# Six places of a two-layer hybrid block rearranged: query norm, last folding, second statistics, context states, head exponents, rotations

## The chip, the cores and the metric

The kernel runs on one core of one Trainium2 chip. A core has five engines that run at once and meet only at semaphores: TensorE (PE; its weight loads are listed apart as PEld), VectorE (DVE), ScalarE (ACT), GpSimd (POOL) and SyncE (SP), which here starts most of the transfers. The metric is the time of one execution on the device in microseconds (us), lower is better; the time before is the median of three runs. All inputs are resident in the device's memory, all arithmetic of the reference is done in the kernel.

## The reference

Two layers of a block with 512 tokens (`x`, width 2048) and 256 context tokens (`ctx`). Each layer modulates a normed input with shift, scale and gate, which come from `silu(c) @ ada_w`; layer 0 mixes a pooling branch and a 12-head attention with low-rank queries and keys (MLA), layer 1 mixes a 4-head bidirectional mLSTM and a 16-head window attention. Cut to what matters here:

```python
for i in range(2):
    shift, scale, gate = split(silu(c) @ ada_w[i] + ada_b[i], 3)         # the context's likewise
    h  = rmsnorm(x,  norm_w[i]) * (1 + scale)   + shift
    hc = rmsnorm(xc, norm_w[i]) * (1 + scale_c) + shift_c
    y, yc = even_mix(h, hc, ...) if i == 0 else odd_mix(h, hc, ...)
    x = x + gate * y
    if i == 0: xc = xc + gate_c * yc
return rmsnorm(x, final_norm)

# even_mix
p_in, p_gate, c_q, c_kv, k_r, a_gate = split(h @ w_in, EV_SIZES)
q = (rmsnorm(c_q, q_norm) @ w_uq)            # 12 heads x (128 + 64 rotated)
k, v from rmsnorm(c_kv, kv_norm) @ w_ukv, k_r rotated
y = concat(pool(p_in) * silu(p_gate), attention(q, k, v) * silu(a_gate)) @ w_out

# odd_mix: the mLSTM starts from the state that the context leaves
C_new = decay * C + einsum('bhs,bhsv,bhsk->bhvk', w, v, k)               # w: gate weights
s     = (q @ k.T) * exp(dlog - m_t)
num   = exp(inter - m_t) * (C @ q) + s @ v
ym    = rmsnorm(num / den) * head_norm * sigmoid(o) * silu(z)
ya    = window_attention(rope(aq), rope(ak), av, ...) * silu(az)
y     = concat(ym, ya) @ w_out
```

## The kernel before

All is computed in float32 with tokens along the free axis. A product of two float32 operands is done as three TensorE products of rounded halves: `split(src, h, l)` has ScalarE write the rounded value `h` and VectorE (or the engine given as `low`) the rest `l = src - h`; `load_w` (L106) brings a piece of weights (raw ring of 3, halves rings of 4) and splits it. `tmode` (L307, L309) and `kmode` (L320) are the matmul loops over four row blocks of 128 of the inner dimension, `kq` in 0..3 over 2048; L307 writes 512 columns of the tokens, L309 256 of the context.

A planner orders each engine's instructions when the program is built: of those that are ready it takes the one that stands first in the program, unless a region marks its work with `tc.high_priority()`, or fixes the order of an engine with `tc.manual_schedule(engines=...)`, where instructions of that engine go out as written. On the chip each queue then runs strictly in the order that was fixed. Tiles come from pools; tiles of one tag share a number of buffers, and a new tile waits for a buffer. PSUM has eight banks; the tag "pm" holds two small tiles in most stages.

**First stage** (about 24 to 590 us): the projection `h @ w_in`, one `in_group` after another. Groups 2 and 3 give `c_q` (768 columns wide); `c_evac` copies them out and sums squares, the copies go to DRAM `cqd`, and only the factor of the norm, `rq`, is kept (L514 to L522). Beside the groups runs `Background`: units of the modulation product, 16 pieces of `ada_w` each, summed by VectorE (L187), transposed and reduced (`red`, L192, L193) and folded over partitions by a small matmul (`pb`, L199) whose result four small VectorE additions place (`ada_place`, L131). The folding of a unit stands 16 steps into the next; that of the last unit stands in `finish`, at the stage's end.

**MLA stage** (about 590 to 1000 us): `cqd` is read back, `c_norm` (L476 on) forms the row factors (`rows`, L253 on: six `dg` products and two copies), multiplies (L480) and splits, with POOL doing the subtractions. Then, under a fixed PE order, heads' scores alternate with fillers (`run(n)`: projections L641, L661 and products of the next stage). `HEAD` is the columns of one head's projection.

**Second layer's input** (about 1000 to 1380 us): output products `out0`, sums of squares, `stats1(0)` (tokens) and `stats1(1)` (context): `stat_mm` (L265), a square root, `rows`. `hx_chunks` is a generator, advanced by `out0`, that writes the normed tokens.

**mLSTM's preparation** (about 1380 to 1560 us): the gates (L1070 to L1185: cumulative sums, per direction `d` a transposition `prow` (L1131), a chain of running maxima on VectorE (L1133 to L1162), `ptr` (L1147) and a transposition back, `pmc` (L1165)); the value products `mv_group(h)`, four pieces `kq` of 72 matmuls (L320) each; and `ctx_state(h, vc)`, which for both directions weighs the context's values (`wv`, L1207), splits them (`wvh`, `wvl`) and multiplies with the context's keys (`pc0`, six matmuls of L1215, printed `pc` in the profile). All small products here share the tag "pm" with two buffers. Last comes the group `odw[5]`. Units 20 to 23 of `Background` run beside it.

**mLSTM heads** (about 1560 to 1840 us): for each head loads and splits (`m_q`, `m_kv`), the output gates' product `m_oz` (192 matmuls into all four "px" banks), then `m_head`: per direction a broadcast product `bc` (one of four "pm" banks), sums and exponentials (`X`, `iw`, `qi`), then scores and the sums over states.

**Window attention** (about 1840 to 2300 us): `wq_split` rotates the queries through `do_rope` (L328 to L335): VectorE swaps halves (`rsw`, L330) and multiplies (`rt1`, L332), POOL multiplies the swapped copy (L334), VectorE adds. ScalarE and VectorE split the result (`wq`, L1436, L1437). The matmuls of projections and of the output (L1449) are fillers beside the heads' scores. `z_load` (L1528 on) reads the mLSTM's result back and splits it: the rounded half on VectorE (L1534), the rest on POOL (L1535).

Of the kernel before, what the change touches and what calls it, by code (L numbers as in the profile page):

```python
# [8 lines left out]
F32 = mybir.dt.float32  # L9
# [29 lines left out]
def tile_hybrid_dit(ctx: ExitStack, tc: tile.TileContext, ts: dict, out: bass.AP, dbg=None, upto=99):  # L39
# [134 lines left out]
    def ada_vec_steps(u, pp, tp, nb, ttag, tbufs):  # L174

        both = u < 20
        acc = [tp.tile([P, 512], F32, name=f"acc{u}_{v}", tag=f"acc{v}", bufs=1) for v in range(2 if both else 1)]
        for kc in range(16):
            at = tp.tile([P, 512], F32, name=f"at{u}_{kc}", tag="ada", bufs=nb)
            DM.dma_start(at, ts["ada"][u, kc // 2][:, (kc % 2) * 512 : (kc % 2) * 512 + 512])  # L180
            if kc == 0:
                V.tensor_scalar(acc[0], at, st[:, kc, 0:1], None, op0=ALU.mult)
                if both:
                    S.mul(acc[1], at, st[:, kc, 1:2])
            else:
                for v, a in enumerate(acc):
                    V.scalar_tensor_tensor(a, at, st[:, kc, v : v + 1], a, op0=ALU.mult, op1=ALU.add)  # L187
            yield
        red = tiny.tile([P, 2, 16], F32, name="red", tag="red", bufs=2)
        for v in range(len(acc)):  # L190
            tr = tp.tile([P, 512], F32, name="atr", tag=ttag, bufs=tbufs)
            V.transpose(tr, acc[v])  # L192
            V.tensor_reduce(red[:, v, :], tr.rearrange("p (b r) -> p b r", r=32), axis=AX.X, op=ALU.add)  # L193
            yield

        def finish():
            n = len(acc)
            pb = pp.tile([32, 2, 16], F32, name=f"pb{u}", tag="pm")
            T.matmul(pb[:, :n, :], fold, red[:, :n, :], start=True, stop=True)  # L199
            ada_place(u, pb, n)  # L200

        return finish

    class Background:
# [5 lines left out]
        def steps(self, units, args):  # L210
            done = None
            for u in units:
                it = ada_vec_steps(u, *args)
                n = 0
                while True:
# [8 lines left out]
                    yield  # L224
            done()

# [3 lines left out]

        def finish(self):
            for _ in self.it:
                pass


# [91 lines left out]
    def do_rope(ps, r, tmp):  # L327

        sw = tmp("rsw", NX)
        V.stream_shuffle(sw, ps[:, :NX], SWAP)  # L330
        t1 = tmp("rt1", NX)
        V.tensor_tensor(t1, ps[:, :NX], rope[0], op=ALU.mult)  # L332
        t2 = tmp("rt2", NX)
# [179 lines left out]

    ssq = [ap_.tile([P, NT], F32, name="ssqc", tag="ssqc", bufs=1), 0]  # L514
    for g in range(2):
        px, pc = in_group(2 + g, steps=(2, 2))
        for b, r in enumerate(c_evac([(px[b], pc[:, b, :]) for b in range(2)], ssq)):
            G.dma_start(cqd[2 * g + b], r)
    p6 = pp.tile([P, 6], F32, name="cps6", tag="pm")
    stat_mm(p6, ssq[0], 6, 512)  # L520
    rq = cp.tile([P, 6], F32, name="rq")
    V.tensor_copy(rq, rstd_col(p6, 6, MLA_SCALE))  # L522

# [63 lines left out]
    for i in range(6):  # L587
# [5 lines left out]
        for b in range(2):  # L593
# [3 lines left out]
            G.dma_start(agd[2 * i + b], t)  # L597
    bg.finish()
    esA.close()
# [24 lines left out]

    raw = []
    for j in range(4):
        raw.append(tf("cqr"))
        DM.dma_start(raw[j], cqd[j])
    c_norm(raw, rq, cq, V_QN, tf, pp, G)

# [197 lines left out]
    with tc.manual_schedule(engines={mybir.EngineType.PE}):  # L828
        run(6 * HEAD + 1024)
        s_stage(units[0], 0)  # L830
        run(HEAD // 4)
        s_stage(units[0], 1)
        run(HEAD // 2)
# [100 lines left out]
    bg.finish()  # L934
    stats1(0)

    def hx_chunks():
        for j in range(KC):
            h_chunk(j, x1[j], ssq1, 12, 1, *((HX[j][i], None) for i in range(2)), Ring(tz, 3), (0,), G if j % 2 else V)
            if j % 4:  # L940
                yield
# [247 lines left out]

    def mv_group(h):  # L1190
        px, pc = new_px(2), new_pc()
        pv = [px[b // 2][:, 256 * (b % 2) : 256 * (b % 2) + 256] for b in range(4)]
        for kq in range(4):
# [4 lines left out]
            bg.step(3)  # L1198
            kmode([pc[:, b, :] for b in range(2)], w, kcs, HC, kq == 0, kq == 3, 2)
        vx_store(h, [p_.rearrange("p (a b) -> p a b", b=256) for p_ in px])  # L1200
        return vc_store([pc])

    def ctx_state(h, vc):
        for d in range(2):
            wv = cm.tile([P, 2, 258], F32, name="wv", tag="wv", bufs=1)
# [3 lines left out]
            wl = cm.tile([P, 2, 258], F32R, name="wvl", tag="wvl", bufs=1)  # L1209
            split(wv, wh, wl)  # L1210
            pc0 = pmt("pc0", [P, 258])
            for b in range(2):
# [4 lines left out]

    ctx_state(0, vc)
    for h in range(1, 4):
        ctx_state(h, mv_group(h))  # L1220

    px, pc = new_px(2), new_pc()
    for kq in range(4):
        w = load_w(odw[5, kq])
        bg.step(2)
        tmode(px, [pc[:, b, :] for b in range(2)], w, range(4 * kq, 4 * kq + 4), HX, HC, kq == 0, kq == 3)
    bg.finish()
# [84 lines left out]

    def m_head(h, q, kv, oz):
        q32, qh, ql = q
        kh, kl, vh, vl = kv
        bcs, Xs, qis = [], [], []
        for d in range(2):
# [14 lines left out]
            Xs.append(X)  # L1332
            qis.append((qih, qil))
        SD = [[], []]
        for s_ in range(4):
# [64 lines left out]
    for h in range(4):  # L1400
        q_, kv_ = m_q(h), m_kv(h)
        m_head(h, q_, kv_, m_oz(h))

# [125 lines left out]
    def z_load(j):  # L1529
        raw = wp.tile([P, 1024], F32, name="wraw", tag="wraw", bufs=3)  # L1530
        for i in range(2):
            DM.dma_start(raw[:, 512 * i : 512 * i + 512], z1d[j + i])
            h, l = Z[j + i]
            V.tensor_copy(h, raw[:, 512 * i : 512 * i + 512])  # L1534
            G.tensor_tensor(l, raw[:, 512 * i : 512 * i + 512], h, op=ALU.subtract)  # L1535

# [326 lines left out]
```

## Time and profile before

| what | value |
|---|---|
| runs shown | 2321.92, 2322.08, 2317.99 us; median 2321.92 |
| profiled execution | 2320.82 us, its span 2319.0 us |
| PE busy | 2232.1 us, 12984 matmuls |
| PEld busy | 1897.7 us |
| DVE busy | 1414.7 us, 2860 instructions |
| ACT busy | 922.0 us, 1872 instructions |
| POOL busy | 177.0 us, 213 instructions |
| moved by DMA | 311.24 MB, mean 134 GB/s |
| mean granted clock | 0.99 |

Busy times are sums over the span of one execution; engines overlap, so they do not add up to it. A row of the waits names the waiting instruction by engine, output tile and line, then the instruction that let it go, then the idle time in total, how often, and the longest. A row of the table by stretches gives for each engine its busy time and number of instructions, then the clock that TensorE was granted as a share of full speed, the DMA engines' share and the rate in GB/s. A row of the timeline gives start, duration, engine, line, operation, out<-in, shape, and in brackets the idle time before it with its releaser. Rows of one line's or tile's instructions give minimum, median and maximum in ns and the first and last start in us.

### The profile page before, as it was taken

The numbers are of one execution on the slowest core, as the hardware profiler recorded it, in microseconds if no ns is written. First come the engines' busy times: TensorE is split into PE (matmuls) and PEld (weight loads), VectorE is DVE, ScalarE is ACT, GpSimd is POOL, SyncE is SP. The second block draws the span as 40 slices with busy tenths as digits, with TensorE's granted clock in tenths as the row PEclk, the third lists the DMA queues.
The fourth block names the chain that finished last, engine by engine and source line by source line (L and its number), as shares of the span: only waits on it lengthen the run. The fifth ranks groups of instructions, "written<-read, shape, count | busy, mean of one in ns | idle before, by whom it ended". The sixth has DMA issues, their size and how long they took to land.

```text
span 2319.0 us, 34267 instructions
## 1 busy us (share of the span) xinstructions
PE 2232.1 (96%) x12984; PEld 1897.7 (82%) x12984; DVE 1414.7 (61%) x2860; ACT 922.0 (40%) x1872; POOL 177.0 (8%) x213
## 2 busy tenths in 40 slices
PE   5999999999899999999999999899999989999997
PEld 3678888788799999878888899898888878776886
DVE  4579432396666766788558525752555676778435
ACT  3232222121344444542225322223565656766433
POOL 0000000000100000011113000000000000003111
PEclk9999999999999999999999999999999999999998
DMA  9856323565211112276444321753233212113434
GB/s 385 320 201 193 111 83 121 198 224 168 78 53 53 58 55 69 96 262 223 151 156 151 96 100 69 255 163 120 93 99 100 96 55 73 64 62 121 136 114 141
DMA packets 118581, 311.24 MB, mean 134 GB/s; under 512 B 13676, under 2 KB 21356, under 8 KB 118416
## 3 DMA queue, kind: packets, MB, share of 16 engines
q1 hardware_dynamic: 111536, 281.73, 36.2%
q0 software_dynamic: 6880, 27.32, 3.1%
q8 instruction: 102, 1.67, 0.3%
q14 instruction: 63, 0.52, 0.1%
HBM read 279.37 MB, written 29.62 MB: 133 GB/s over the span
## 4 chain that ended last, share of the span: by engine, by line
PE 62%; DVE 6%; DMA 2%; issue 2%; ACT 1%; POOL 0%; DVEq 0%; SPq 0%; ACTq 0%; POOLq 0%
PE px L307 17%; PE px L320 10%; PE pj L641 5%; PE px L1449 5%; PE s L704 4%; PE pc L309 3%; PE om L747 3%; PE pc L320 2%; PE s L1449 2%; PE pj L661 2%; PE po L1368 2%; PE tp L729 2%; DMA at<-in_ada_dram 1%; PE wpt L1611 1%; DVE wl L109 1%
## 5 line engine op out<-in xcount | busy, mean ns | idle before, releaser
L108 ACT CAST wh<-wraw 128x512 fp32r<-128x512 f32 (+2 forms) x556 | 326.4, 591 | 881.3 <-PE pc L309 407.1
L109 DVE TENSOR_TENSOR wl<-wraw,wh 128x512 fp32r<-128x512 f32 (+2 forms) x556 | 371.2, 673 | 491.6 <-ACT wh L108 472.0
L187 DVE SCALAR_TENSOR_TENSOR acc<-at,st,acc 128x512 f32<-128x512 f32 x360 | 253.2, 755 | 23.6 <-DMA at<-in_ada_dram 22.5
L320 PE MATMUL px<-wh,hxh 128*128 128x512 f32 (+2 forms) x512 | 175.0, 342 | 0.0
L320 PE MATMUL px<-wl,hxh 128*128 128x512 f32 (+2 forms) x512 | 174.3, 340 | 0.0
L320 PE MATMUL px<-wh,hxl 128*128 128x512 f32 (+2 forms) x512 | 174.2, 340 | 0.0
L307 PE MATMUL px<-h0h,wh 128*128 128x512 f32 x384 | 153.0, 398 | 0.0
L307 PE MATMUL px<-h0h,wl 128*128 128x512 f32 x384 | 151.7, 395 | 0.1
L307 PE MATMUL px<-h0l,wh 128*128 128x512 f32 x384 | 151.7, 395 | 0.0
L309 PE MATMUL pc<-h0h,wl 128*128 128x256 f32 x400 | 112.6, 282 | 0.0
L309 PE MATMUL pc<-h0h,wh 128*128 128x256 f32 x400 | 112.4, 281 | 0.0
L309 PE MATMUL pc<-h0l,wh 128*128 128x256 f32 x400 | 112.4, 281 | 0.0
L320 PEld LDWEIGHTS px<-wh,hxh 128*128 128x128 f32 x512 | 96.8, 189 | 12.5 <-ACT sz L1292 1.0
L320 PEld LDWEIGHTS px<-wl,hxh 128*128 128x128 f32 x512 | 96.8, 189 | 11.3
L320 PEld LDWEIGHTS px<-wh,hxl 128*128 128x128 f32 x512 | 96.9, 189 | 11.0
L307 PEld LDWEIGHTS px<-h0h,wh 128*128 128x128 f32 x384 | 72.1, 188 | 23.1 <-ACT wh L108 4.2
L307 PE MATMUL px<-hxh,wh 128*128 128x512 f32 x224 | 89.5, 400 | 0.0
L307 PE MATMUL px<-zxl,wh 128*128 128x512 f32 x224 | 89.3, 399 | 0.0
L307 PE MATMUL px<-hxl,wh 128*128 128x512 f32 x224 | 89.2, 398 | 0.0
L307 PE MATMUL px<-hxh,wl 128*128 128x512 f32 x224 | 89.2, 398 | 0.0
L307 PE MATMUL px<-zxh,wl 128*128 128x512 f32 x224 | 88.7, 396 | 0.0
L307 PE MATMUL px<-zxh,wh 128*128 128x512 f32 x224 | 88.3, 394 | 0.0
(880 smaller groups left out, 6020.9 us busy)
## 6 DMA issues: line engine op xcount, KB each, us to landing
at<-in_ada_dram SPq DMA_DIRECT2D x256, 256.0 KB, 3.4
at<-in_ada_dram SPq DMA_DIRECT2D x64, 512.0 KB, 7.9
wraw<-in_od_in_dram SPq DMA_DIRECT2D x64, 512.0 KB, 3.5
wraw<-in_ev_in_dram SPq DMA_DIRECT2D x56, 512.0 KB, 4.2
wraw<-in_ev_out_dram SPq DMA_DIRECT2D x44, 512.0 KB, 3.9
wraw<-in_od_out_dram SPq DMA_DIRECT2D x36, 512.0 KB, 3.5
wraw<-in_od_oz_dram SPq DMA_DIRECT2D x32, 512.0 KB, 3.5
xt<-in_xT_dram SPq DMA_DIRECT2D x16, 384.0 KB, 7.4
```

Source lines behind the costliest of these rows:

```text
L108: S.copy(h, src)
L109: low.tensor_tensor(l, src, h, op=ALU.subtract)
L187: V.scalar_tensor_tensor(a, at, st[:, kc, v : v + 1], a, op0=ALU.mult, op1=ALU.add)
L307: T.matmul(px[b], w_, Hx[kc][r_], start=s0, stop=s1)
L309: T.matmul(pc[b], w_, Hc[kc][r_], start=s0 and b == 0, stop=s1, skip_group_check=True)
L320: T.matmul(p_, h_, w_, start=s0, stop=s1, skip_group_check=True)
L641: T.matmul(t, w_, r_[:, sl], start=kc == 0 and n == 0, stop=kc == 3 and n == 2)
L661: T.matmul(t[:, b * 256 : (b + 1) * 256], h_, w_, start=kc == 0 and n == 0 and b == 0, stop=kc == 3 and n == 2, skip_group_check=True)
L704: T.matmul(s[:, c0 - k0 : c1 - k0], l_, r_[:, c0:c1], start=n == 0, stop=n == 4)
L729: T.transpose(tp[:, b * P : (b + 1) * P], pr[:, (b0 + b) * P : (b0 + b + 1) * P], ident)
L747: T.matmul(o[:, :256], v_[:, 6 - nk + b, :], p_[:, b, :], start=b == 0 and n == 0, stop=b == nk - 1 and n == 2)
L1449: T.matmul(px[b], w_, Hs[kc][r_], start=first and i == 0 and n == 0, stop=last and i == len(kcs) - 1 and n == 2)
```

## The change

- **Query norm**: in the first stage, behind group 3, `rows` is called and the four products with `q_norm` are done in place on the copies in `raw`; only then do they go to `cqd`. The MLA stage loads them and splits them, with VectorE as `low`.
- **Last folding**: `finish` of `Background` can leave the last unit's folding out; it is called by `bg.last(pp)` behind the first quarter of a head's filler in the MLA stage, with that stage's PSUM pool.
- **Second statistics**: `stats1(0)` moves from ahead of the last three output products into `hx_chunks`, which first advances behind the first `kq` of the first of them.
- **Context states**: `ctx_state` becomes a generator that stops ahead of each direction's products. `mv_group` advances the state of the head before behind `kq` 0 and `kq` 2, and so does the group `odw[5]` for the last head. These groups and the states' products stand under a fixed PE order, as written.
- **Head exponents**: the first half of `m_head` becomes `m_pre`, called before `m_oz`.
- **Rotations**: the swap and the first product of `do_rope` are marked with high priority.
- Besides, `z_load` splits with ScalarE and VectorE in place of VectorE and POOL.

```diff
@@ -193,9 +193,9 @@
             V.tensor_reduce(red[:, v, :], tr.rearrange("p (b r) -> p b r", r=32), axis=AX.X, op=ALU.add)
             yield
 
-        def finish():
+        def finish(pool=None):
             n = len(acc)
-            pb = pp.tile([32, 2, 16], F32, name=f"pb{u}", tag="pm")
+            pb = (pool or pp).tile([32, 2, 16], F32, name=f"pb{u}", tag="pm")
             T.matmul(pb[:, :n, :], fold, red[:, :n, :], start=True, stop=True)
             ada_place(u, pb, n)
 
@@ -222,15 +222,17 @@
                     if n == 16 and done:
                         done()
                     yield
-            done()
+            self.last = done
 
         def step(self, n=1):
             for _ in range(n):
                 next(self.it, None)
 
-        def finish(self):
+        def finish(self, fold=True):
             for _ in self.it:
                 pass
+            if fold:
+                self.last()
 
 
     def rstd_col(ps6, nb, mul=None, bufs=2):
@@ -327,9 +329,10 @@
     def do_rope(ps, r, tmp):
 
         sw = tmp("rsw", NX)
-        V.stream_shuffle(sw, ps[:, :NX], SWAP)
         t1 = tmp("rt1", NX)
-        V.tensor_tensor(t1, ps[:, :NX], rope[0], op=ALU.mult)
+        with tc.high_priority():
+            V.stream_shuffle(sw, ps[:, :NX], SWAP)
+            V.tensor_tensor(t1, ps[:, :NX], rope[0], op=ALU.mult)
         t2 = tmp("rt2", NX)
         G.tensor_tensor(t2, sw, rope[1], op=ALU.mult)
         V.tensor_tensor(r[:, :NX], t1, t2, op=ALU.add)
@@ -512,14 +515,16 @@
 
 
     ssq = [ap_.tile([P, NT], F32, name="ssqc", tag="ssqc", bufs=1), 0]
+    raw = []
     for g in range(2):
         px, pc = in_group(2 + g, steps=(2, 2))
-        for b, r in enumerate(c_evac([(px[b], pc[:, b, :]) for b in range(2)], ssq)):
-            G.dma_start(cqd[2 * g + b], r)
+        raw += c_evac([(px[b], pc[:, b, :]) for b in range(2)], ssq)
     p6 = pp.tile([P, 6], F32, name="cps6", tag="pm")
     stat_mm(p6, ssq[0], 6, 512)
-    rq = cp.tile([P, 6], F32, name="rq")
-    V.tensor_copy(rq, rstd_col(p6, 6, MLA_SCALE))
+    rb = rows(rstd_col(p6, 6, MLA_SCALE), 6, pp, ta("rstdb"))
+    for j in range(4):
+        V.scalar_tensor_tensor(raw[j], raw[j], vec[:, V_QN + j : V_QN + j + 1], rb, op0=ALU.mult, op1=ALU.mult)
+        G.dma_start(cqd[j], raw[j])
 
 
     m = NP - 16
@@ -595,7 +600,7 @@
             S.activation(t[:, :NX], px[b], AF.Silu)
             S.activation(t[:, NX:], pc[:, b, :], AF.Silu)
             G.dma_start(agd[2 * i + b], t)
-    bg.finish()
+    bg.finish(fold=False)
     esA.close()
     es0.close()
 
@@ -622,11 +627,10 @@
     def tf(name, n=NT):
         return mp.tile([P, NT], F32, name=name, tag="tf", bufs=11)[:, :n]
 
-    raw = []
     for j in range(4):
-        raw.append(tf("cqr"))
-        DM.dma_start(raw[j], cqd[j])
-    c_norm(raw, rq, cq, V_QN, tf, pp, G)
+        r = tf("cqr")
+        DM.dma_start(r, cqd[j])
+        split(r, *cq[j])
 
     heads = [dict() for _ in range(12)]
 
@@ -829,6 +833,7 @@
         run(6 * HEAD + 1024)
         s_stage(units[0], 0)
         run(HEAD // 4)
+        bg.last(pp)
         s_stage(units[0], 1)
         run(HEAD // 2)
         for i, un in enumerate(units):
@@ -932,9 +937,9 @@
     hxp = opool(ehx, "hx", side="right")
     HX = [(hxp.tile([P, NX], F32R, name=f"hxh{j}"), hxp.tile([P, NX], F32R, name=f"hxl{j}")) for j in range(KC)]
     bg.finish()
-    stats1(0)
 
     def hx_chunks():
+        stats1(0)
         for j in range(KC):
             h_chunk(j, x1[j], ssq1, 12, 1, *((HX[j][i], None) for i in range(2)), Ring(tz, 3), (0,), G if j % 2 else V)
             if j % 4:
@@ -1187,7 +1192,7 @@
     bg = Background(range(20, 24), pp, opool(ea, "ada1"), 4, "atr", 1)
 
 
-    def mv_group(h):
+    def mv_group(h, state):
         px, pc = new_px(2), new_pc()
         pv = [px[b // 2][:, 256 * (b % 2) : 256 * (b % 2) + 256] for b in range(4)]
         for kq in range(4):
@@ -1197,10 +1202,13 @@
             kmode(pv, w, kcs, HX, kq == 0, kq == 3, 2)
             bg.step(3)
             kmode([pc[:, b, :] for b in range(2)], w, kcs, HC, kq == 0, kq == 3, 2)
+            if kq % 2 == 0:
+                next(state, None)
         vx_store(h, [p_.rearrange("p (a b) -> p a b", b=256) for p_ in px])
         return vc_store([pc])
 
     def ctx_state(h, vc):
+
         for d in range(2):
             wv = cm.tile([P, 2, 258], F32, name="wv", tag="wv", bufs=1)
             for b in range(2):
@@ -1208,6 +1216,7 @@
             wh = cm.tile([P, 2, 258], F32R, name="wvh", tag="wvh", bufs=1)
             wl = cm.tile([P, 2, 258], F32R, name="wvl", tag="wvl", bufs=1)
             split(wv, wh, wl)
+            yield
             pc0 = pmt("pc0", [P, 258])
             for b in range(2):
                 kh, kl = (m_[:, b, h * P : (h + 1) * P] for m_ in mkc)
@@ -1215,15 +1224,22 @@
                     T.matmul(pc0, k_, w_[:, b, :], start=b == 0 and n == 0, stop=b == 1 and n == 2)
             split(pc0, C0[4 * d + h][0], C0[4 * d + h][1])
 
-    ctx_state(0, vc)
-    for h in range(1, 4):
-        ctx_state(h, mv_group(h))
+    state = ctx_state(0, vc)
+    next(state)
+    with tc.manual_schedule(engines={mybir.EngineType.PE}):
+        for h in range(1, 4):
+            vc = mv_group(h, state)
+            state = ctx_state(h, vc)
+            next(state)
 
     px, pc = new_px(2), new_pc()
     for kq in range(4):
         w = load_w(odw[5, kq])
         bg.step(2)
-        tmode(px, [pc[:, b, :] for b in range(2)], w, range(4 * kq, 4 * kq + 4), HX, HC, kq == 0, kq == 3)
+        with tc.manual_schedule(engines={mybir.EngineType.PE}):
+            tmode(px, [pc[:, b, :] for b in range(2)], w, range(4 * kq, 4 * kq + 4), HX, HC, kq == 0, kq == 3)
+            if kq % 2 == 0:
+                next(state, None)
     bg.finish()
     ea.close()
     for b in range(2):
@@ -1310,9 +1326,8 @@
             split(vr, vh[:, 2 * b : 2 * b + 2, :256], vl[:, 2 * b : 2 * b + 2, :256])
         return kh, kl, vh, vl
 
-    def m_head(h, q, kv, oz):
-        q32, qh, ql = q
-        kh, kl, vh, vl = kv
+    def m_pre(h, q32):
+
         bcs, Xs, qis = [], [], []
         for d in range(2):
             bc = pm4("bc", [P, 512])
@@ -1331,6 +1346,12 @@
             bcs.append(bc4)
             Xs.append(X)
             qis.append((qih, qil))
+        return bcs, Xs, qis
+
+    def m_head(h, q, kv, pre, oz):
+        q32, qh, ql = q
+        kh, kl, vh, vl = kv
+        bcs, Xs, qis = pre
         SD = [[], []]
         for s_ in range(4):
             sc = pm4("sc", [P, 512])
@@ -1399,7 +1420,7 @@
 
     for h in range(4):
         q_, kv_ = m_q(h), m_kv(h)
-        m_head(h, q_, kv_, m_oz(h))
+        m_head(h, q_, kv_, m_pre(h, q_[0]), m_oz(h))
 
     for b, px in enumerate(x_group_t(G_AQ)):
         S.copy(aq0[b], px)
@@ -1531,8 +1552,7 @@
         for i in range(2):
             DM.dma_start(raw[:, 512 * i : 512 * i + 512], z1d[j + i])
             h, l = Z[j + i]
-            V.tensor_copy(h, raw[:, 512 * i : 512 * i + 512])
-            G.tensor_tensor(l, raw[:, 512 * i : 512 * i + 512], h, op=ALU.subtract)
+            split(raw[:, 512 * i : 512 * i + 512], h, l)
 
     def fillers():
```

## The prediction

> **What bounds the kernel now.** The profile page comes first: how long the span is and which engine fills it.
>
> ```profile
> span 2319.0 us, 34267 instructions
> PE 2232.1 (96%) x12984; PEld 1897.7 (82%) x12984; DVE 1414.7 (61%) x2860; ACT 922.0 (40%) x1872; POOL 177.0 (8%) x213
> ```
>
> TensorE (PE) is busy for 2232.1 of 2319.0 us and nothing else passes 61% apart from its own weight loads. So the end moves by what PE waits for, and by the clock it runs at, and by little else. Work taken off VectorE (DVE), ScalarE (ACT) or GpSimd (POOL) is worth something only where PE waits for it. The second view is the list of PE's waits (instruction, releaser; total us, times, longest):
>
> ```profile
> PE ps L265 <- DVE rb L392: 23.4, 1, 23.4
> PE pc L1215 <- ACT wvh L108: 6.6, 2, 6.2
> PE px L1449 <- ACT az L1407: 4.2, 1, 4.2
> PE pj L641 <- DVE vl L109: 3.2, 1, 3.2
> PE pb L199 <- DVE red L193: 3.1, 1, 3.1
> PE ps6b L265 <- DVE ssq L885: 3.0, 1, 3.0
> PE px L1449 <- DVE rt L332: 1.9, 1, 1.9
> ```
>
> The 23.4 us are the start-up and are not touched. The next six are 22.0 us in all (6.6 + 4.2 + 3.2 + 3.1 + 3.0 + 1.9), under 1% of the span. A wait has a tail, though. The table by stretches, cut from PE's restart after each, shows it (start and end, us, busy of PE, PEld, DVE, ACT, POOL, then the granted clock):
>
> ```profile
> 591.20:597.00 5.80, 5.80 (x28) 5.74 (x29) 2.37 (x9) 0.00 (x0) 0.00 (x0) 0.51 1.00 357
> 610.20:614.00 3.80, 3.80 (x16) 3.51 (x17) 1.60 (x4) 1.08 (x3) 1.19 (x1) 0.55 0.21 69
> 1507.20:1511.70 4.50, 4.44 (x21) 4.44 (x22) 3.49 (x8) 0.83 (x3) 0.00 (x0) 0.51 0.90 277
> 1870.30:1873.50 3.20, 3.17 (x11) 2.68 (x12) 0.69 (x1) 0.77 (x2) 0.00 (x0) 0.51 0.26 63
> 1909.50:1914.50 5.00, 4.96 (x17) 3.92 (x18) 4.90 (x10) 3.77 (x6) 0.00 (x0) 0.66 0.19 50
> ```
>
> PE is full in each, at about half clock. Length times (1 - clock) is lost: 5.8 x 0.49 = 2.8, 3.8 x 0.45 = 1.7, 4.5 x 0.49 = 2.2, 3.2 x 0.49 = 1.6, 5.0 x 0.34 = 1.7 us. I count these 10.0 us as part of the waits. The Trainium skill (TensorE: Matmul & The Clock Gate, "HAM oscillation — how this bites in real kernels") asks for no idle gap of TensorE over about 3.4 us. By that rule the gaps of 3.1, 3.2 and 1.9 us would leave no tail, and 2.8 + 1.7 + 1.7 = 6.2 us of gain would drop out of the sum. The trace disagrees: the clock falls behind each of them, so the measurement decides.
>
> **Query norm.** PE's 3.2 us wait is for a value split `vl`, and DVE's timeline shows why that is late:
>
> ```profile
> 606.01 3.68 DVE L109 TENSOR_TENSOR wl<-wraw,wh 128x256 fp32r<-128x256 f32 x2
> 609.61 0.41 DVE L109 TENSOR_TENSOR vl<-pj,vh 128x256 fp32r<-128x256 f32 x1
> 602.48 8.91 POOL L109 TENSOR_TENSOR cql<-cnt,cqh 128x768 fp32r<-128x768 f32 x4 [12.34 <-ACT cqh L108]
> L480 DVE SCALAR_TENSOR_TENSOR cnt<-cqr,vec,rstdb x4: 1007/1008/1981, 600.0 to 603.8; 128x768 f32<-128x768 f32 x4
> ```
>
> Two `wl` take 3.68 us while POOL runs the four `cql` subtractions; the `vl` after them takes 0.41. Before that stand four `cnt` products of 1.0 to 2.0 us. The change moves the products, with the row statistics (six small matmuls, two copies), into the first stage, and gives the subtractions to DVE. There the moved work has room:
>
> ```profile
> 240.00:258.00 18.00, 18.00 (x107) 15.65 (x107) 9.72 (x23) 2.79 (x6) 1.26 (x2) 1.00 0.52 170
> 1227.00:1235.00 8.00, 7.73 (x64) 7.38 (x63) 4.89 (x12) 3.65 (x6) 0.00 (x0) 1.00 0.49 168
> ```
>
> DVE is busy 9.72 of 18 us where four products of 1.0 us and two copies are added; PE is full and goes on with the next group. I cost it at nothing; without that cover it is at most those four products plus copies, about 5 us. The four `cqd` stores now follow the norm, but they are read 350 us later. At the MLA stage DVE has four subtractions of estimated 1.0 us (an operation of that size, L480, takes 1.0) in place of four products of 1.0 to 2.0, with POOL silent. `vl` then comes before PE needs it: **-3.2 - 1.7 = -4.9**.
>
> **Last unit's folding.** The 3.1 us wait goes, since the fold matmul stands after a quarter head of filler. Next late is the PSUM bank of the gate group, on which PE's next product lands:
>
> ```profile
> 588.40 0.65 ACT L596 ACTIVATE sag<-pc 128x256 f32<-128x256 f32 x2
> ```
>
> It is read until 589.05, and PE is out of matmuls at 588.0: some 1.1 us stay, too short for a tail by the rows above. **-2.0 - 2.8 = -4.8**. Its four small additions now run on DVE at a point where it is not late.
>
> **Second statistics.** The call moved is that of the first half (near 1232 us). There PE is busy 7.73 of 8 us (row of 1227 above), so nothing is to be won; the wait of 3.0 us (`ps6b`) belongs to the second half's call, which stays. **0**, within 1 us either way.
>
> **Context states.** The 6.2 us wait with its tail goes: in the new order PE runs another quarter of the next group (72 matmuls; 0.124 us each by the row of L320 below, 8.9 us) before the state's product, while `wvh` was 6.2 late. **-6.6 - 2.2 = -8.8.** But the PE order is now fixed from the first state on: three quarters of group 1 stand behind the product of state 0. Rows of the gates' last transposes (L1165) and of that product (L1215: count, durations, first and last start), then of single instructions:
>
> ```profile
> L1165 PE MATMUL pmc<-con,Mr x8: 198/219/225, 1435.3 to 1449.4; 4*128 4x4 f32 x8
> L1215 PE MATMUL pc<-wvh,mkch x16: 282/335/583, 1449.5 to 1548.8; 128*128 128x258 f32 x16
> 1424.01 0.62 ACT L108 CAST wvh<-wv 128x516 fp32r<-128x516 f32 x1 [2.32 <-DVE wv L1207]
> 1424.79 0.68 DVE L109 TENSOR_TENSOR wvl<-wv,wvh 128x516 fp32r<-128x516 f32 x1
> 1426.80 0.19 DVE L1113 TENSOR_TENSOR rho<-II,beta 128x32 f32<-128x32 f32 x1
> 1429.27 0.14 DVE L1149 COPY tr<-ptr 4x4 f32<-4x4 f32 x1
> 1435.48 0.60 PE L1131 MATMUL prow<-con,rho 128*4 128x128 f32 x4
> 1449.20 0.41 PE L1165 MATMUL pmc<-con,Mr 4*128 4x4 f32 x4
> ```
>
> State 0's operands are ready at 1425.5, yet its product runs at 1449.54, right behind the last `pmc`. In the same way the second direction's `prow`, whose input is ready at 1427.0 and for which both buffers are free from 1429.41, runs at 1435.48, right behind the first `pmc`. All are tiles of one PSUM tag with two buffers. I read it as: that tag hands out its buffers in the order of the program, so state 0's product cannot start before the last `pmc`, which ends DVE's chain of running maxima. In before PE fills that time with group 1:
>
> ```profile
> 1431.00:1449.50 18.50, 17.14 (x138) 16.13 (x136) 1.00 0.21 72
> ```
>
> (matmuls of L320 alone). These 17.1 us of work (17.14 / 138 = 0.124 us each) would now stand behind the product. DVE could end its chain up to 2.7 us sooner, as four `wl` splits of that engine (0.67 each, as the `wvl` row above) lie within it; so 14.4 to 17.1, I take 15, and 2 for the clock after it (the tails above are 1.6 to 2.8). The other end is no cost at all, if the buffer comes free early. I take the stall, since two instructions show the same pattern. **+17 - 8.8 = +8.2.**
>
> **Head exponents.** They move ahead of the head's gate products. PE has no gap there:
>
> ```profile
> 1580.00:1840.00 260.00, 259.85 (x1283) 213.87 (x1283) 138.03 (x314) 146.14 (x365) 7.77 (x25) 1.00 0.30 99
> ```
>
> 0.15 us idle in 260. Nothing to win; two of four small PSUM buffers are held longer, which could cost up to 1.5 us. **0.**
>
> **Rotations.** The chain ahead of the 4.2 us wait:
>
> ```profile
> 1860.14 0.68 DVE L332 TENSOR_TENSOR rt<-aq,rope 128x512 f32<-128x512 f32 x1
> 1862.57 1.79 DVE L332 TENSOR_TENSOR rt<-aq,rope 128x512 f32<-128x512 f32 x1
> 1866.62 1.26 ACT L1436 CAST wq<-wrr 64x512 fp32r<-64x512 f32 x2 [2.62 <-DVE wrr L335]
> 1867.89 1.28 ACT L1407 ACT_TABLE_LOAD   x1
> 1869.19 1.09 ACT L1407 ACTIVATE az<-px 128x512 f32<-128x512 f32 x2
> 1908.81 0.68 DVE L332 TENSOR_TENSOR rt<-px,rope 128x512 f32<-128x512 f32 x1
> ```
>
> `rt` waits in DVE's queue, slowed to 1.79 beside POOL; `wrr`, `wq` follow, and ACT reaches the table load and `az`, which frees PE's bank, only after `wq`. With the shuffle and the product first in the queue the second `rt` would follow the first at once and without POOL beside it (1860.8 and 0.68 against 1862.57 and 1.79, 2.9 us sooner), and the first comes sooner too. I take 3.2: 4.2 becomes about 1.0 and the tail goes, **-3.2 - 1.6**. At 1907 the product could run at 1907.5 in place of 1908.81: **-1.3**, and half of the 1.7 tail, since about 0.6 of wait stays. Sum **-7**, between -4 and -9.
>
> **Last loads** (`z_load`). DVE casts and POOL subtracts; now ACT casts and DVE subtracts.
>
> ```profile
> 2093.00:2125.00 32.00, 26.49 (x125) 19.12 (x124) 29.57 (x53) 19.80 (x38) 19.71 (x14) 1.00 0.43 140
> L1535 POOL TENSOR_TENSOR z1l<-wraw,z1h x14: 1289/1446/1806, 2092.9 to 2121.6; 128x512 fp32r<-128x512 f32 x14
> L1534 DVE CAST z1h<-wraw x14: 411/424/1534, 2092.4 to 2120.1; 128x512 fp32r<-128x512 f32 x14
> ```
>
> PE idles 5.5 of 32 us, DVE is at 29.57. Casts of median 0.42 but up to 1.53 become subtractions of 0.67: 14 x 0.25 = 3.5 us more by median, but nothing slows DVE any more; ACT takes on 14 x 0.62 = 8.7 beside 19.8. I take **-3.5**, between -5.5 and +1.
>
> **Sum.** -4.9 - 4.8 + 0 + 8.2 + 0 - 7 - 3.5 = -12.0. The profiled execution took 2320.82 us (span 2319.0 and 1.8 around it), so 2308.8; the median of the runs is 1.1 higher: 2310.
>
> **Rivals.**
> A: no stall at state 0. The tag's order is inferred from two coincidences. If the buffer comes free at 1441, or the planner puts the product elsewhere, 17 falls away: -29, **2293**. For it: PE's order within the fixed part says nothing of work outside it.
> B: slower. With PE's order fixed, nothing fills in where a state's operands are late, as DVE's queue waits for the background weights of `bg.step`. The stall at state 0 then comes at its upper end (17.1 + 2.8 = 19.9) and the eight products share another stand of the size of the old tail and half the old wait, 5; the 8.8 are won. In part four that is +16.1, and the rest gives back only what its sure members hold: 4.9 + 4.8 = 9.7, with rotations and last loads at +0. Net +6.4: **2328**. It decides from where part four costs more than the others win, 20.2 by the sum above and 9.7 in this case. Against it: six of the eight products are not late today (6.6 us in 2 waits).
> C: it does not do what it says. Each wait is replaced by the next one half as long (the bank at 589, ACT at 1870), z_load gives nothing: -(4.9 + 4.8 + 7) / 2 + 8.2 = -0.2, **2322**.
>
> **Chances.** Forecast 0.42, A 0.35, B 0.12, C 0.11. The forecast's own range is 2304 to 2316. 8 in 10 reach from A's lower side (2289; last loads at -5.5, rotations at -9) to just above C (2324), which leaves B out. Faster by over 0.2% (4.6 us, about what can be told from no change here): forecast and A, 0.77. C, with a slice of B, is "same": 0.12. Slower 0.11.
>
> **What would show it.** Right: no wait at `pj` and `pb` over 1.5 us near 590 and 610, clock 1.0 there; a PE gap of 13 to 17 us near 1431 to 1449 ahead of `pc` L1215; none at 1500; `wq` near 1863. Wrong: matmuls of L320 all through 1431 to 1449 (rival A), gaps ahead of other states' products (B), `ps6b` L265 no longer waiting near 1279, which I hold untouched.

## The result, and the profile after

The changed kernel takes 2337.93 us (median of four runs, 2337.43 to 2340.46), the kernel before 2322.0 in the same runs: a ratio of 1.0068, interval 1.0056 to 1.008. It is 0.7% slower. The forecast was 2310, and 2324 the upper end of its range. The page of the changed kernel begins:

```profile
span 2336.1 us, 34264 instructions
PE 2233.2 (96%) x12984; PEld 1898.5 (81%) x12984; DVE 1409.2 (60%) x2863; ACT 933.0 (40%) x1889; POOL 147.5 (6%) x195
```

PE does the same 12984 matmuls in the same busy time (2233.2 against 2232.1 us) and ends 17.1 us later: all of the difference is waiting and clock. The longest of PE's waits in the changed kernel, apart from the start-up, as before (instruction, releaser; total, times, longest):

```profile
PE pmc L1170 <- DVE Mr L1158: 9.0, 3, 8.1
PE px L1470 <- ACT z1h L108: 5.5, 1, 5.5
PE px L309 <- DVE x L881: 5.1, 1, 5.1
PE ps6b L267 <- DVE ssq L890: 4.7, 2, 4.4
PE pmc L1170 <- DVE BI L1185: 3.9, 1, 3.9
PE pc L1224 <- ACT wvh L108: 3.7, 2, 3.4
PE s L1514 <- DVE wm L1519: 2.5, 2, 1.9
PE px L322 <- ACT sz L1308: 2.3, 3, 0.8
```

The waits for `red`, `az` and `rt` are gone, those for `vl` and `wvh` smaller, that for `ps6b` has grown, and six new ones stand beside it (`wm` had 0.2 us before). A list of waits doesn't say what each costs in the end, because a later wait can absorb an earlier delay. So both traces were laid side by side by matmul work: for each point of the kernel before, how much later the changed kernel has done the same sum of matmul columns. This table is worked out from the two traces' matmuls (us; minus is ahead):

```
before at    550    650   1000   1050   1300   1400   1450   1550   1850   1900   1950   2050   2100   2150    end
lag         +1.9   -7.7   -3.9   +1.5   +2.8   +2.8  +18.6  +15.0  +20.1  +14.4  +11.9  +12.5  +20.7  +17.0  +17.1
```

From 550 to 650 the lag falls by 9.6 us (query norm and folding). Most of the first 1.9 is work done early that comes back: the lag at 550 is mostly the six `dg` products, not time lost. So the first two parts stand at a lead of 7.7 us, where the forecast had 9.7. Between 650 and 1000 3.8 are lost in small pieces, and near 1005 another 5.4. Between 1431 and 1450 15.8 go, and near 1500 only 3.6 come back. 5 are lost over the four heads and 6 won at 1866, 2.5 won at 1907, and 8 lost and 4 won again between 2058 and 2140.

The stretch at 1434, by stretches and then PE's timeline (columns as in the prediction; the first row of all instructions, the second of L322 alone):

```profile
1433.80:1450.20 16.40, 2.78 (x20) 1.37 (x20) 15.80 (x67) 0.62 (x1) 0.13 (x2) 0.61 0.13 48
1433.80:1450.20 16.40, 0.34 (x3) 0.13 (x2) 0.61 0.13 48
```

```profile
1433.86 0.28 PE L322 MATMUL pc<-wh,hcl 128*128 128x256 f32 x1
1438.07 0.23 PE L1170 MATMUL pmc<-con,Mr 4*128 4x4 f32 x1 [3.92 <-DVE BI L1185]
...
1450.10 0.58 PE L1170 MATMUL pmc<-con,Mr 4*128 4x4 f32 x4 [8.10 <-DVE Mr L1158]
1450.61 0.58 PE L1224 MATMUL pc<-wvh,mkch 128*128 128x258 f32 x1
```

Where the kernel before ran 138 matmuls of the next group, the changed one runs three. Its product of state 0 comes right behind the last `pmc`, while VectorE is busy for 15.8 of 16.4 us, nearly all of it with the gates and their chain of running maxima.

### The profile page after: what moved, and what is told of

Read it like the earlier page. It is cut to its first block, busy times and chain, and to the rows that moved or that the text cites. A ratio compares the mean times of both kernels' runs of the same rounds, so it can differ in the third digit from the quotient of the medians.

```text
span 2336.1 us, 34264 instructions
## 1 busy us (share of the span) xinstructions
PE 2233.2 (96%) x12984; PEld 1898.5 (81%) x12984; DVE 1409.2 (60%) x2863; ACT 933.0 (40%) x1889; POOL 147.5 (6%) x195
## 4 chain that ended last, share of the span: by engine, by line
PE 82%; DVE 9%; ACT 3%; DMA 3%; issue 2%; POOL 0%; SPq 0%; DVEq 0%; ACTq 0%; POOLq 0%
PE px L309 29%; PE pc L311 9%; PE px L322 9%; PE pj L645 5%; PE px L1470 5%; PE s L708 4%; PE om L751 2%; PE px L381 2%; PE s L1470 2%; PE pc L322 2%; PE pj L665 2%; DMA at<-in_ada_dram 2%; PE po L1389 2%; PE tp L733 2%; PE pa L143 1%
## 5 line engine op out<-in xcount | busy, mean ns | idle before, releaser
L322 PE MATMUL px<-wh,hxh 128*128 128x512 f32 (+2 forms) x512 | 175.4, 343 | 2.3 <-ACT sz L1308 2.3
L322 PE MATMUL px<-wl,hxh 128*128 128x512 f32 (+2 forms) x512 | 174.4, 341 | 0.0
L322 PE MATMUL px<-wh,hxl 128*128 128x512 f32 (+2 forms) x512 | 174.2, 340 | 0.0
L322 PEld LDWEIGHTS px<-wh,hxh 128*128 128x128 f32 x512 | 97.5, 190 | 15.5 <-ACT sz L1308 3.6
L322 PEld LDWEIGHTS px<-wh,hxl 128*128 128x128 f32 x512 | 97.3, 190 | 11.6
L322 PEld LDWEIGHTS px<-wl,hxh 128*128 128x128 f32 x512 | 97.3, 190 | 10.9
```

The costliest lines, as they stand in the source:

```text
L322: T.matmul(p_, h_, w_, start=s0, stop=s1, skip_group_check=True)
```

## The experiments

All are judged by their ratio to the kernel before, run on the same chip, since chips differ by some 2 us; where places are compared, it is by the work done, as in the table above.

**State 0 outside the fixed order.**

```diff
-    state = ctx_state(0, vc)
-    next(state)
+    for _ in ctx_state(0, vc):
+        pass
+    state = iter(())
     with tc.manual_schedule(engines={mybir.EngineType.PE}):
```

> The changed kernel, except that state 0 runs to its end ahead of the fixed PE order, as before the change; the other three states stay interleaved. Theory (the idle stretch at 1434 to 1450 is the price of state 0's product standing inside the fixed order, behind the last pmc): the gap of 12 to 16 us ahead of L1224 is gone, matmuls of L322 fill 1434 to 1450, and the time falls from 2337.9 by 14 to 17, to about 2322. Rival (the stretch is the running-maxima chain itself, which holds up PE wherever the product stands): the gap stays, 2337.

Measured: 2318.48 us, ratio 0.9981 (0.9972 to 0.999). The stretch is full again:

```profile
1433.80:1450.20 16.40, 16.40 (x140) 15.50 (x140) 15.83 (x65) 2.49 (x4) 0.13 (x2) 1.00 0.17 51
```

By the work done this run gains 15.8 us on the changed kernel between 1400 and 1450, and nothing of size elsewhere; the medians differ by 20 us, and the profiled execution was the slowest of its ten. VectorE's chain is as long as it was (15.83 us busy), so the chain alone stops nobody.

**Another PSUM tag for the product.**

```diff
-            pc0 = pmt("pc0", [P, 258])
+            pc0 = pp.tile([P, 258], F32, name="pc0", tag="pc")
```

> The changed kernel with one word changed: the states' product pc0 takes a buffer of the PSUM tag pc in place of pm; the fixed order is as in the changed kernel. Theory (PE waits because the pm tag hands out its two buffers in program order, so pc0 comes behind the last pmc): pc0 runs at the end of kq 0, near 1434, well ahead of pmc, the gap is gone, about 2322. Rival (PE waits because of the fixed order or of the operands wvh, wvl): pc0 still comes behind pmc or waits as long, 2337.

Measured: 2320.03 us, ratio 0.9986 (0.9976 to 0.9996). The fixed order is that of the changed kernel, but the product now runs at 1431.9, ahead of the first `pmc` (rows of L1224 and L1170: count, durations in ns, first and last start):

```profile
L1224 PE MATMUL pc<-wvh,mkch x16: 279/285/385, 1431.9 to 1568.6; 128*128 128x258 f32 x16
L1170 PE MATMUL pmc<-con,Mr x8: 198/220/225, 1436.1 to 1450.9; 4*128 4x4 f32 x8
```

So it was neither the operands nor the fixed order alone, but that order together with a tag that hands out its buffers as the program names them. The gain up to 1450 is about 16 us again; 5.3 are given back at the last group's end, where the next `pc` waits for the last state's buffer:

```profile
PE pc L311 <- DVE c0l L109: 3.5, 1, 3.5
```

**A `pm` tile first in the MLA stage's pool.**

```diff
+    V.memset(new_pm("first")[0:1, 0:1], 0.0)
     esM = ExitStack()
```

> The changed kernel with a small pm tile written first in the MLA stage's PSUM pool (one added memset), so that pm takes the pool's first banks, as it did when the row factors of the query norm were formed there. Theory (the new wait of 5.1 us ahead of px L309 at 1002 comes from the banks: without a pm tile ahead of it pj takes the first banks, and the next stage's first px falls on the bank that the second x L881 still has to read): that wait is gone, 5 us less, about 2333. Rival (the wait comes from VectorE being late with x by its queue alone): it stays, 2338.

Measured: 2333.31 us, ratio 1.0042 (1.0027 to 1.0057), against 1.0068. The wait for `x` near 1002 is gone, and by the work done the run gains 6.9 us there. One small tile, used for nothing, is worth that. (In the run with five repairs, which has the same tile, a wait of 2.0 us for `x` is left there; why is not shown.)

**The query norm alone, on the kernel before** (the edit of the change, none of its other parts).

> The kernel before with the query norm moved, alone. Theory (the wait for vl and its tail, 4.9 us, are won; but pj then is the first tile in the MLA stage's pool, and the next stage's first px meets it: a new wait for x near 1005 of 5 to 7 us): within 2 us of before, with both in the trace. Rival (the new wait belongs to another part of the change): 5 us less than before, no wait for x.

Measured: 2323.54 us, ratio 1.0004 (0.9995 to 1.0014). Both are there: by the work done the run is 1.7 us late at 550 (the products done early), 6.9 ahead at 650, with 4.7 of it won between 600 and 650, and late again by 2.2 at 1050, with 9.3 lost on the way. The lead of 6.9 is more than the 4.9 forecast for this part. The wait for `red` stands here as before, with 3.1 us, but no half clock follows it: the granted clock is 1.00 in the row behind it.

```profile
PE pb L199 <- DVE red L193: 3.1, 1, 3.1
592.90:600.00 7.10, 7.10 (x60) 7.06 (x61) 3.31 (x9) 3.17 (x6) 0.00 (x0) 1.00 0.89 315
```

The new wait, on PE's timeline of this run:

```profile
1008.19 0.77 PE L307 MATMUL px<-zxh,wh 128*128 128x512 f32 x1 [7.14 <-DVE x L877]
```

With the row factors formed in the first stage, `pj` is the first tile of the MLA stage's pool. Then the next stage's first `px` has to wait until VectorE has read the second `pj` (`x`, at 1006.54 in the changed kernel). That the two share PSUM banks in this case, and did not in the kernel before, is concluded from these two edits; the trace names no banks.

**`z_load` as before** (cast on VectorE, subtraction on GpSimd, in place of the `split`).

> The changed kernel with z_load as before (rounded half on VectorE, rest on GpSimd). Theory (ScalarE's queue: z1h at 2114.8 stands behind twelve softmax activations while its data landed near 2104, so the new split costs time): the wait of 5.5 us at px<-z1h near 2110 is gone and the 1.4 us of waits for z1l come back; 3 to 5 us less than the changed kernel, 2333 to 2335. Rival (the predicted gain of 3.5 is there and the wait at 2110 has another cause): 3 us more, 2341.

Measured: 2337.84 us, ratio 1.0063 (1.0048 to 1.0078): neither forecast. The wait of 5.5 us is gone, and the small ones are back (waits between 2030 and 2150):

```profile
PE wpo L1643 <- DVE wpl L109: 3.9, 4, 1.4
PE s L1514 <- DVE wm L1519: 2.7, 3, 1.9
PE px L1470 <- POOL z1l L1556: 1.4, 3, 0.5
```

3.9 + 1.4 = 5.3 us against 5.5: the new split is worth nothing either way, and the loss at 2058 isn't its doing.

**Head exponents behind `m_oz`.**

```diff
-        m_head(h, q_, kv_, m_pre(h, q_[0]), m_oz(h))
+        oz_ = m_oz(h)
+        m_head(h, q_, kv_, m_pre(h, q_[0]), oz_)
```

> The changed kernel with the head exponents (m_pre) called behind m_oz, as before the change. Theory (ahead of m_oz they leave PE only score products to run while ScalarE loads its tables and empties the four px banks, so PE waits four times about 0.8 us for sz, and some more): the waits for sz L1308 are gone and the stretch 1600 to 1868 is 4 to 5 us shorter, 2333. Rival (the 5 us of that stretch come from something else, such as the store of z1 and the loads of the next head): within 1 us of the changed kernel.

Measured: 2340.29 us, ratio 1.0079 (1.0063 to 1.0096), not faster at all. The waits for `sz` are gone and 5.3 us are won between 1600 and 1850. But then the old wait stands again, some 7 us with its tail, although the rotations still have their priority:

```profile
PE px L1471 <- ACT az L1429: 4.3, 1, 4.3
```

VectorE's rows of this run show why the priority doesn't help there:

```profile
1865.12 1.79 DVE L335 TENSOR_TENSOR rt<-aq,rope 128x512 f32<-128x512 f32 x1
...
1868.17 0.95 DVE L1600 TENSOR_TENSOR KLw<-kro,KHw 64x768 fp32r<-64x768 f32 x1
...
1873.99 0.69 DVE L338 TENSOR_TENSOR wrr<-rt,rt 128x512 f32<-128x512 f32 x1
...
1875.20 1.80 DVE L335 TENSOR_TENSOR rt<-aq,rope 128x512 f32<-128x512 f32 x1
```

The first product is early, but its sum `wrr` has kept its old place behind the splits of the keys (`KLw`), and the second product comes 10 us after the first, behind `wrr`: `rt1` has one buffer (`rtmp` with `bufs=1`), which `wrr` frees.

**The first statistics as before** (`stats1(0)` ahead of the last output products).

> The changed kernel with stats1(0) ahead of the last three output products, as before the change. Theory (the later statistics push the first chunks and with them the last x L881 back behind VectorE's queue, so the wait ahead of ps6b near 1278 grew from 3.0 to 4.4 us, with more time at half clock): about 2.5 us less, 2335.5. Rival (the wait is set by the transfer of xr, as before): no difference.

Measured: 2339.47 us, ratio 1.008 (1.0064 to 1.0095). No difference; the wait ahead of `ps6b` is 4.5 us here too. Its growth from 3.0 isn't due to the moved statistics.

**The priority for two groups of queries only** (`high_priority` in `do_rope` behind a flag, off for the last two groups).

> The changed kernel with the high priority of do_rope kept for the first two groups of queries of the window attention only (and the MLA's), and taken from the last two. Theory (in the last group swap and product go ahead of the softmax maximum on VectorE, and PE's wait for wm near 2069, 2.5 us, is its price): that wait shrinks to the 0.2 us of before, 3 to 4 us less, 2334. The early gain near 1866 to 1914 stays. Rival (wm is late for another reason): no difference.

Measured: 2336.11 us, ratio 1.0061 (1.0048 to 1.0075). The wait for `wm` is gone, and 3.8 us are won between 2050 and 2100 by the work done, as expected; the medians show half of it. In the changed kernel VectorE's rows at that place are:

```profile
2067.86 0.74 DVE L334 STREAM_SHUFFLE rsw<-px 128x512 f32<-128x512 f32 x1
2068.49 0.67 DVE L335 TENSOR_TENSOR rt<-px,rope 128x512 f32<-128x512 f32 x1
2069.09 1.21 DVE L1650 TENSOR_TENSOR wzt<-wzt,wzg 128x256 f32<-128x256 f32 x1
2070.22 0.68 DVE L1519 CUSTOM_DVE_ANT_0 wpr__20730<-s,msk 128x512 f32<-128x512 f32 x1
```

The softmax maximum (L1519), on which PE's next scores wait, stands behind a rotation that nobody needs yet.

**The rotations' priority alone, on the kernel before.**

> The kernel before with the high priority in do_rope alone. Theory (formed after the run with the head exponents put back, where the wait of 4.3 us for az stood again although the priority was there: the second rt cannot start before wrr has freed the one rt1 buffer, and wrr kept its place behind the KHw and KLw operations): the wait for az L1407 near 1866 stays at 4 us, the one for rt near 1907 goes (2 to 3 us with its tail), the wait for wm near 2058 grows by 2 to 4 us; in sum within 2 us of before. Rival (the prediction: priority takes the wait at 1866 away): 5 to 7 us less than before.

Measured: 2329.81 us, ratio 1.0034 (1.0021 to 1.0046): slower, outside both expectations. By the work done, -2.5 us at 1907 and +3.8 at 2058 as expected; about 3 us more between 1450 and 1550, where the wait for `wvh` is 7.0 us here and 6.2 before; and 2.2 between 650 and 900, in five steps of 0.4 to 0.5, in the MLA stage, which rotates its queries through the same function. New small waits for the softmax's `pr` and `rs` stand at four of them, and the one for `knl` has grown by 0.5 at the other. The wait for `az` is as it was:

```profile
PE px L1450 <- ACT az L1408: 4.6, 1, 4.6
```

**The last folding as before** (`bg.finish()`, no `bg.last`).

> The changed kernel with the last unit's folding back ahead of the MLA stage. Theory (the moved folding is worth its wait and its tail, 4.8 us): a wait of 3 us for red ahead of pb near 588 with half clock behind it, 4 to 5 us more than the changed kernel, 2342; the small waits of the MLA stage (0.4 us each at five places) stay. Rival (the moved folding causes those small waits, 3 us in sum): they go, 1 to 2 us more.

Measured: 2342.39 us, ratio 1.0085 (1.0071 to 1.0099), 0.0017 or 4 us above the changed kernel; the intervals of the two ratios overlap. By the work done it is 2.5 us later at 650. The wait for `red` is back with 3.1 us, and the granted clock is 0.79 from 591.20 to 597.00, where the kernel before had 0.51. The small waits of the MLA stage stay.

**Five repairs at once** (state 0 outside, `pm` first, statistics and head exponents as before, priority for two groups).

> The changed kernel with five repairs at once: state 0 outside the fixed order, a pm tile first in the MLA stage's pool, stats1(0) and the head exponents as before, the priority of the rotations for the first two groups only. z_load stays as changed. Theory (the pieces add up: 2337.9 - 16 - 6 - 2.5 - 4.5 - 3.5): 2303 to 2309, some 0.7% below the kernel before. Rival (each repair only moves a wait to the next engine): above 2314.

Measured: 2311.83 us, ratio 0.995 (0.9936 to 0.9964). Faster than before, but 6 us above the middle of what was expected: the wait for `az` is back (4.5 us and its tail).

**Three more priorities on top of the five repairs** (`wv`, `wvh` and `wvl`; the split of `z_load`; the sum `wrr` for two groups).

> The kernel of the five repairs with three priorities more: the weighing and splitting of the context's values (wv, wvh, wvl), the split in z_load, and the last sum of do_rope for the first two groups. Theory (PE's waits of 3.4 us for wvh, 5.5 for z1h and 4.5 for az are each work that stands late in an engine's queue although its data are there): these three go with their tails, 8 to 14 us below the 2311.8 of the five repairs, 2298 to 2304. Rival (queue time is only exchanged: softmax or background weights are late instead): 2308 to 2313.

Measured: 2318.36 us, ratio 0.9977 (0.9966 to 0.9989): worse than the rival had it, and by the ratios some 6 us slower than the five repairs. `wvh` is at 2.7 us, `z1h` is gone, but ScalarE is now late with the next output gate, and `az` is no better:

```profile
PE px L1476 <- ACT wzg L1495: 4.8, 2, 3.9
PE px L1476 <- ACT az L1434: 4.7, 1, 4.7
```

VectorE's rows show how far the prioritized sum helps:

```profile
1845.26 0.67 DVE L339 TENSOR_TENSOR wrr<-rt,rt 128x512 f32<-128x512 f32 x1
...
1846.54 1.68 DVE L335 TENSOR_TENSOR rt<-aq,rope 128x512 f32<-128x512 f32 x1
...
1854.65 1.41 DVE L1464 TENSOR_TENSOR wq<-wrr,wq 64x512 fp32r<-64x512 f32 x2
...
1856.16 0.69 DVE L339 TENSOR_TENSOR wrr<-rt,rt 128x512 f32<-128x512 f32 x1
```

The second product now follows the first sum at once. But `wrr` has one buffer too, which the split `wq` frees, and `wq` has kept its place behind the keys' splits. `az` starts at 1859.46 in place of 1862.48 with the five repairs, 3.0 us sooner, but PE comes there 3.3 us sooner as well (1855.88 against 1859.16), so its wait stays.

**Five repairs with a single prioritized group, `z_load` as before; and the same with the head exponents early.**

> The five repairs, and besides z_load as before and the priority of the rotations for the second group of the window attention's queries alone. Theory (the priority costs 0.3 us each at four places of the MLA stage and 3.8 us near 2069 and is worth 2.5 us near 1907; z_load is worth nothing either way): the waits for pr near 657, 720, 783, 846 and for wm near 2069 are gone, and 3 to 6 us less than with the five repairs, 2306 to 2309 on a chip where before takes 2322. If the wait ahead of ps6b near 1278 falls back to 3.0 us, it belonged to the priority. Rival (the repairs only exchange waits): 2311 or more.

> The same, with the head exponents ahead of m_oz as in the changed kernel. Theory (PE comes 5 us later through the four heads, so it meets the rotated queries' chain, which VectorE paces, with no wait: 4.5 us for az and its tail are exchanged against about as much in the heads): no wait for az, 1.2 us more in each of four heads, in sum within 1.5 us of the run without it. Rival (the head exponents' place removes the wait by itself): 4 us less.

Measured: 2308.17 us, ratio 0.9931 (0.9917 to 0.9945), and 2306.13 us, ratio 0.9923 (0.9909 to 0.9937). The first has no wait for `pr` or `wm` above 0.2; `az` is at 4.2. The second has no wait for `az`; by the work done it loses 5.3 us to the first from 1600 to 1850 and wins 6.6 between 1850 and 1900. `az` starts at about the same time in both (1858.44 and 1858.74). So the head exponents' new place only makes PE come later to a chain that VectorE paces; the 2 us between the medians lie within the two intervals. This last kernel keeps the query norm, the folding, three of the four states, the head exponents and one rotation, and is 0.8% faster than the kernel before.

## Why the prediction was wrong

**What bounds the kernel: right. The tails: right in part.** PE's busy time did not move, and where a wait of the list went, its half clock went too: the granted clock is 1.00 in this row of the changed kernel, and 0.51 stood from 591.20 to 597.00 before.

```profile
587.00:597.00 10.00, 9.15 (x70) 8.52 (x69) 3.82 (x12) 2.92 (x8) 1.07 (x2) 1.00 0.49 167
```

But a tail doesn't belong to its wait as firmly as the sum took it: behind the same 3.1 us at `pb` the clock is 0.51 before, 0.79 with the folding put back, and 1.00 with the norm alone.

**Query norm and folding, -9.7: nearly right where they stand** (a lead of 7.7 us at 650), **but split otherwise:** the norm alone leads by 6.9 where 4.9 were forecast, and the folding adds 2.5 by the work done, or 4 by the medians, where it was 4.8. At 590 0.9 us of wait are left, close to the 1.1 that were expected, though by the profile for `av` and not for the bank. **The norm's step failed by what it left out.** It said that the moved work lies beside other work and costs nothing. It did not ask which tile is the first in the stage's PSUM pool once the row factors are formed elsewhere. That costs 5.4 us in the changed kernel, 7.1 of wait with the norm alone, where it takes the whole gain.

**Second statistics, 0: right.** Putting them back changes nothing. The wait of the context's statistics, which was held untouched, grew by 1.4 us. Every run with more than one part has it grown, whichever part was undone. What causes it is open.

**Context states: the stall was right, +15.8 for 17**, at the place, the length and by the cause that was given; both edits that remove the cause remove it. **The gain of 8.8 was mis-sized: it is 3.6.** It took the operands to be ready once another quarter group (8.9 us) lay ahead of the product. VectorE's queue holds `wv` behind the background sums that wait for their transfers, and in the new place PE still waits 3.4 and 0.8 us, with a tail (1524 to 1532, clock 0.85):

```profile
1522.42 3.16 DVE L187 SCALAR_TENSOR_TENSOR acc<-at,st,acc 128x512 f32<-128x512 f32 x4 [1.36 <-DMA at<-in_ada_dram]
...
1526.87 0.61 DVE L1215 TENSOR_SCALAR wv<-vcx,wcol 128x258 f32<-128x258 f32 x2
```

In the five runs with state 0 outside the order the same stretch, 1450 to 1550, gives 4.5 to 6.2 us. The net is +12 where the prediction had +8.

**Head exponents, 0: right in sum, wrong in the reading.** PE was full there, and filling it otherwise cost 5 us over the four heads. They came back at 1866.

**Rotations, -7: wrong.** "The second `rt` would follow the first at once" was the step. It looked at the queue and not at the one buffer of `rt1`, nor at `wrr`, which kept its old place. VectorE's row between the two `rt` of the kernel before already had it:

```profile
1861.38 0.68 DVE L335 TENSOR_TENSOR wrr<-rt,rt 128x512 f32<-128x512 f32 x1
```

At 1866 the priority does nothing; at 1907 it wins 2.5; at 2058 it costs 3.8 and in the MLA stage some 2. Alone it makes the kernel slower.

**Last loads, -3.5: wrong.** The prediction priced the split by VectorE's time and set ScalarE's 8.7 us more beside its busy share. It didn't look at ScalarE's order. `z1h` is cast at 2114.80, behind the activations of the softmax, about 10 us after its data were there (transfers issued at 2100.49, 3.2 us to landing). And its list of waits passed over the third row in size of the kernel before:

```profile
2114.80 1.65 ACT L108 CAST z1h<-wraw 128x512 fp32r<-128x512 f32 x3
PE wpo L1622 <- DVE wpl L109: 4.5, 6, 1.4
```

The first row is of the changed kernel. The second is what the new split wins (1.6 us are left of it) and pays for with the wait for `z1h`.

**The rivals.** A (no stall) fell. B gave the right sign at 2328, yet its mechanism (one more stall among the states) isn't what happened: the other states do not stand longer. The 28 us between forecast and result are, by the work done: 2 by which the lead at 650 falls short, 5.4 at 1005, 4 at the states, some 10 at the rotations (-7 expected; -2.5, +3.8 and +2 found, 0 at 1866 after the heads' 5 are set against it), 3.5 at the last loads, and some 3 in small waits, the grown `ps6b` among them, that no run isolates.

## What to carry to other kernels

Before work is put into an order written by hand, ask for every tile in it which buffer it takes, and what the program names ahead of it under the same tag: a fixed order turns a harmless allocation in program order into a stop of the whole engine. When the first tile of a pool moves to another stage, the next stage's waits can move with it. And a priority given inside a helper acts on all its callers: look for the one chain that is late, and follow it through every tile with a single buffer to the instruction that frees it, before marking a part of it. No run here marks the whole chain.

## What the runs showed of the hardware

A wait of 1.9 us can be followed by a lowered clock: in the kernel before, the one near 1907 was followed by 5 us at 0.66. But the length of a wait alone doesn't decide it: one of 3.1 us, in the run with the query norm alone, was followed by 7.1 us at 1.00. What decides it, no run here shows. Idle time that comes in pieces cost only itself in the changed kernel's four heads, where PE idles 4.2 of 262 us in pieces of 0.8 us and less and the clock stays at 1.00:

```profile
1606.00:1868.00 262.00, 257.83 (x1270) 211.93 (x1269) 136.44 (x316) 147.07 (x360) 8.13 (x21) 1.00 0.29 96
```
